# Element order of the squares in a group norm: from the token order to the order of the DRAM row

## The chip, the core and the metric

The kernel runs on one core of a Trainium2 chip. The metric is the device time of one execution in microseconds (us), from the first to the last instruction and what lies around it. The engines named below are TensorE (PE; its loads of the stationary operand are listed apart as PEld), VectorE (DVE), ScalarE (ACT), GpSimd (POOL) and SyncE (SP, which issues DMAs).

## The reference, cut to what matters

One decoder block: two token mixers (dilated attention, and a Mamba-2 state-space mixer), a gated merge, and an MLP, for 512 tokens of width 1024 in float32. The change touches the end of the state-space mixer, where the output of each of 8 groups (256 channels) is gated, and normalised by the mean of its squares over the 256 channels of the group:

```python
y = y.reshape(b, s, SSM_INNER) * jax.nn.silu(z.astype(jnp.float32))
yg = y.reshape(b, s, SSM_GROUPS, SSM_INNER // SSM_GROUPS)
yg = yg * lax.rsqrt(jnp.mean(yg * yg, axis=-1, keepdims=True) + RMS_EPS)
y = yg.reshape(b, s, SSM_INNER) * norm_w.astype(jnp.float32)
```

## The kernel before, in words

All projections run on TensorE, with both operands split into a rounded part ("h") and a rest ("l"), as three matmuls per 128x128 block of weights: 128 rows by 512 tokens each. TensorE executes its instructions in the order of the program: `mm` and `tr` (lines 227 and 230) pin every one.

The state-space mixer takes the 8 groups in turn. `ssm_group(g, sz)` is a generator of seven steps; the loop that drives it puts matmuls of the next projections (`fill`: x, B and C, z, and the output projection of the group before) between two steps, a fixed number of them. In the fourth step of a group, for each half j of its channels (128 channels on the partitions, 512 tokens in the free dimension), DVE makes the gated output y (lines 831 to 839) and ACT writes its squares, divided by 256, to a tile q (line 841). DVE adds the two tiles of squares into the first (line 844). Then come 10.5 us worth of other matmuls by the kernel's own count (`SSM_FILL`), and in the fifth step TensorE sums the squares over the partitions: four matmuls whose stationary operand is 128 of the 512 columns of squares and whose moving operand is one column of ones, so that the sums land in a PSUM tile `pn` with 128 tokens on the partitions and 4 columns. Each of these float32 matmuls is two instructions in the trace, and each has a load of its own: 64 loads and 64 matmuls in the 8 groups.

Column c of `pn` holds the tokens 4t + c, t being the partition: so the stationary operand of column c is every fourth element of the 512 (`by4`). The order is there for what follows: DVE adds epsilon to `pn` (line 212), POOL raises it to the power -1/2 (line 215), a DMA writes the [128, 4] tile to a row in DRAM, where t and c together are the token in order, and a second DMA reads that row back to all partitions, where DVE scales y by it (line 864).

ACT's squares are pinned to the order of the program, as are all of TensorE's instructions. Where the addition on DVE (line 844) and the evacuations around it stand on their engines is the scheduler's choice.

Of the kernel before, what the change touches and what calls it, by code (L numbers as in the profile page):

```python
# [13 lines left out]
AF = mybir.ActivationFunctionType  # L14
# [4 lines left out]
P = 128  # L19
T = 512  # L20
NT = 4
# [16 lines left out]
UC = 256  # L38
# [45 lines left out]
def hybrid_block(ctx: ExitStack, tc: tile.TileContext, a: dict):  # L84
    nc = tc.nc
    act, dve, pool, pe, sp = nc.scalar, nc.vector, nc.gpsimd, nc.tensor, nc.sync
# [8 lines left out]
    def split(src, hi, lo, eng=None, pinned=False, lo_pinned=False):  # L95
        ins = act.activation(hi, src, AF.Copy)  # L96
        if pinned:
            tc.keep_in_program_order(ins)
        ins = (eng or dve).tensor_tensor(lo, src, hi.bitcast(F32), op=ALU.subtract)  # L99
        if lo_pinned:  # L100
            tc.keep_in_program_order(ins)
# [107 lines left out]
    def rstd_of(dst, ms, ms2=None):  # L209

        if ms2 is None:
            dve.tensor_scalar(dst, ms, EPS, None, ALU.add)
        else:
            dve.tensor_scalar(dst, ms, ms2, EPS, ALU.add, ALU.add)
        pool.tensor_tensor(dst, dst, mhalf.broadcast_to(list(dst.shape)), op=ALU.pow)

    ones = const.tile([P, P], F32, name="ones")
# [5 lines left out]
    def pin(ins):  # L223
        return tc.keep_in_program_order(ins)

    def mm(*args, **kw):
        tc.keep_in_program_order(pe.matmul(*args, **kw))  # L227

    def tr(dst, src):
        tc.keep_in_program_order(pe.transpose(dst, src, ident))  # L230
# [4 lines left out]
    def three(ps, wh, wl, uh, ul, start, stop, w_moving=False):  # L235
        if w_moving:
            mm(ps, uh, wh, start=start, stop=False)
            mm(ps, uh, wl, start=False, stop=False)
            mm(ps, ul, wh, start=False, stop=stop)
        else:  # L240
            mm(ps, wh, uh, start=start, stop=False)
            mm(ps, wh, ul, start=False, stop=False)
            mm(ps, wl, uh, start=False, stop=stop)
# [14 lines left out]
    def abank(name):  # L258
        return psa.tile([P, T], F32, name=name, tag="a")
# [18 lines left out]
    with tc.tile_pool(name="start", bufs=1, reuse_waits="tile") as st:  # L278
# [163 lines left out]
        t = [vp.tile([P, GROUPS, NT, HG], F32, name=f"dt{j}") for j in range(4)]  # L442
# [185 lines left out]
    for key in ATT_UNITS:  # L628
        n, j = key[:-1], int(key[-1])
# [70 lines left out]
    def bc64(t, g, c0=0, c1=NT):  # L700
        v = t[:, g * 16 + c0 * HG : g * 16 + c1 * HG]
        return v.unsqueeze(2).broadcast_to([P, (c1 - c0) * HG, 64])

    def h64(ap_):
        return ap_.rearrange("p (q e) -> p q e", e=64)
# [62 lines left out]
    def ssm_group(g, sz):  # L768

        xs2 = [convs.pop((g, c)) for c in range(2)]  # L770
        w, e = ws_e.pop(g)

        xd = sg.tile([P, NT * UC], F32, name=f"xd{g}", tag="xd")
        for b in range(2):
            pt = abank(f"ptx{g}_{b}")
            for c2 in range(2):
                c = 2 * b + c2
                for j, xx in enumerate(xs2):
                    tr(pt[:, c2 * UC + j * P : c2 * UC + (j + 1) * P], xx[:, c * P : (c + 1) * P])
            dve.tensor_tensor(h64(xd[:, b * T : (b + 1) * T]), h64(pt), bc64(dtc, g, 2 * b, 2 * b + 2), op=ALU.mult)  # L780
        xs = sg.tile([P, 3 * UC], F32, name=f"xs{g}", tag="prev")
        dve.tensor_tensor(h64(xs), h64(xd[:, : 3 * UC]), bc64(ds_, g, 0, 3), op=ALU.mult)
        xsp = [sg.tile([P, 3 * UC], F32R, name=f"xs{n}{g}", tag=f"xs{n}") for n in "hl"]
        split(xs, *xsp)
        yield

        bt, ct = convs.pop((g, 2)), convs.pop((g, 3))
        pb = abank(f"pb{g}")
        for c in range(3):
            tr(pb[:, c * P : (c + 1) * P], bt[:, c * P : (c + 1) * P])  # L790
        bk = [sg.tile([P, TC], F32R, name=f"bk{n}{g}", tag=f"bk{n}") for n in "hl"]
        split(pb[:, :TC], *bk)
        pcb = abank(f"pcb{g}")
        for c in range(NT):
            cs = slice(c * P, (c + 1) * P)
            mm(pcb[:, cs], bt[:, cs], ct[:, cs], start=True, stop=True)
        cbm = sg.tile([P, NT, P], F32, name=f"cbm{g}", tag="cbm")
        dve.tensor_tensor(cbm, pcb.rearrange("p (c l) -> p c l", c=NT), tri.unsqueeze(1).broadcast_to([P, NT, P]),
                          op=ALU.mult)
        for c in range(NT):  # L800
            wv = w[:, c * HG : (c + 1) * HG, :]
            dve.tensor_tensor(wv, wv, cbm[:, c, :].unsqueeze(1).broadcast_to([P, HG, P]), op=ALU.mult)
        yield

        prev = sg.tile([P, 3, UC], F32, name=f"prev{g}", tag="prev")
        pst = [abank(f"pst{g}_{b}") for b in range(2)]
        for c in range(3):
            pv = pst[c // 2][:, (c % 2) * UC : (c % 2 + 1) * UC]
            bs, us = slice(c * P, (c + 1) * P), slice(c * UC, (c + 1) * UC)
            three(pv, bk[0][:, bs], bk[1][:, bs], xsp[0][:, us], xsp[1][:, us], True, True)  # L810
        with tc.high_priority(offset=200):
            act.activation(prev[:, 0, :], pst[0][:, 0:UC], AF.Copy)
            for c in (1, 2):
                pv = pst[c // 2][:, (c % 2) * UC : (c % 2 + 1) * UC]
                pin(dve.tensor_tensor(h64(prev[:, c, :]), h64(prev[:, c - 1, :]), bc64(cd, g, c, c + 1), op=ALU.mult))
                pin(dve.tensor_tensor(prev[:, c, :], prev[:, c, :], pv, op=ALU.add))
        while held:
            held.pop()()
        yield

        ys, sq = [], []
        pyds = [abank(f"pyd{g}_{j}") for j in range(2)]
        for j in range(2):
            for c in range(NT):
                for half in range(2):
                    h = 2 * j + half
                    mm(pyds[j][64 * half : 64 * half + 64, c * P : (c + 1) * P],
                       xd[:, c * UC + h * 64 : c * UC + (h + 1) * 64], w[:, c * HG + h, :], start=True, stop=True)
        for j in range(2):
            y = sg.tile([P, T], F32, name=f"y{g}_{j}", tag="y", bufs=2)  # L830
            dve.scalar_tensor_tensor(y, xs2[j], dskip[:, 2 * g + j : 2 * g + j + 1], pyds[j], op0=ALU.mult, op1=ALU.add)
            pyo = abank(f"pyo{g}_{j}")
            for c in range(1, NT):
                mm(pyo[:, (c - 1) * P : c * P], prev[:, c - 1, j * P : (j + 1) * P], ct[:, c * P : (c + 1) * P],
                   start=True, stop=True)
            t1 = sg.tile([P, TC], F32, name=f"t1{g}_{j}", tag="t1", bufs=2)
            dve.tensor_tensor(t1, pyo[:, :TC], e[:, j, :], op=ALU.mult)
            dve.tensor_tensor(y[:, P:], y[:, P:], t1, op=ALU.add)
            dve.scalar_tensor_tensor(y, y, 0.5, sz[j], op0=ALU.mult, op1=ALU.mult)
            q = sg.tile([P, T], F32, name=f"sq{g}_{j}", tag="sq", bufs=2)  # L840
            pin(act.activation(q, y, AF.Square, scale=1.0 / math.sqrt(UC)))
            ys.append(y)
            sq.append(q)
        dve.tensor_tensor(sq[0], sq[0], sq[1], op=ALU.add)
        yield

        pn = abank(f"pn{g}")
        by4 = sq[0].rearrange("p (t c) -> p c t", c=NT)
        for c in range(NT):
            mm(pn[:, c : c + 1], by4[:, c, :], ones[:, 0:1], start=True, stop=True)  # L850
        rt = sg.tile([P, NT], F32, name=f"rt{g}", tag="rt", bufs=2)
        rstd_of(rt, pn[:, :NT])

        row = dram.tile([P, NT], F32, name=f"rt_d{g}")
        pool.dma_start(row, rt)
        rstd = sg.tile([P, T], F32, name=f"rg{g}", tag="rg")
        pool.dma_start(rstd, row.rearrange("(o t) c -> o (t c)", o=1).broadcast_to([P, T]))
        if g + 1 < GROUPS:
            decays(g + 1)
        yield  # L860
        yield
        yt = yts[g] = [sg.tile([P, 2, T], F32R, name=f"yt{n}{g}", tag=f"yt{n}", bufs=1) for n in "hl"]
        for j in range(2):
            pin(dve.scalar_tensor_tensor(ys[j], ys[j], nw[:, 2 * g + j : 2 * g + j + 1], rstd,
                                         op0=ALU.mult, op1=ALU.mult))
            split(ys[j], yt[0][:, j, :], yt[1][:, j, :])
# [501 lines left out]
```

## Time and profile before

| | |
|---|---|
| median of 3 runs | 1097.21 us (1097.13 to 1097.43) |
| the profiled execution | 1096.37 us |
| its span, first to last instruction | 1094.5 us |
| TensorE matmuls, share of the span | 99% |
| TensorE loads, share of the span | 85% |
| DVE, ACT, POOL, share of the span | 67%, 48%, 7% |
| mean granted clock of TensorE | 0.998 |

[...] What a stretch costs is read from the starts of its instructions.

### The profile page before, as it was taken

How to read it: one execution, taken by the hardware profiler on the slowest of the kernel's cores; microseconds unless marked ns; L12 is line 12 of the kernel's file. 1: busy time of each engine (PE TensorE's matmuls, PEld its weight loads, DVE VectorE, ACT ScalarE, POOL GpSimd, SP SyncE). 2: the span in 40 equal slices, each digit the busy share in tenths (PEclk: the TensorE clock that was granted, in tenths of full speed). 3: DMA queues.
4: the chain of work that ended last, by engine and by line, in shares of the span. 5: the costliest groups of instructions: out<-in, count | busy, mean ns of one | idle time of the engine just before them, and what ended most of it. 6: DMA issues, size and time to landing. Idle time of an engine off the chain costs nothing.

```text
span 1094.5 us, 14714 instructions
## 1 busy us (share of the span) xinstructions
PE 1083.4 (99%) x5959; PEld 929.5 (85%) x5959; DVE 730.9 (67%) x1088; ACT 527.9 (48%) x921; POOL 72.0 (7%) x87
## 2 busy tenths in 40 slices
PE   9999999999999999999999999999999999999997
PEld 8988887778888888888888878889899998888886
DVE  6557666446776879696969695868677886243324
ACT  6256656435374645546373623443467666232322
POOL 3203122000000000000000000000000000000000
PEclk9999999999999999999999999999999999999999
DMA  8232112323333332323324222560233323333202
GB/s 278 81 116 78 55 63 68 106 68 106 116 87 119 84 125 78 125 82 121 112 92 150 86 82 88 191 192 1 78 116 116 102 93 135 116 118 113 80 37 78
DMA packets 87653, 113.06 MB, mean 103 GB/s; under 512 B 4624, under 2 KB 74768, under 8 KB 86560
## 3 DMA queue, kind: packets, MB, share of 16 engines
q1 hardware_dynamic: 85216, 101.01, 28.7%
q0 software_dynamic: 2224, 11.09, 3.0%
q8 instruction: 47, 0.77, 0.3%
q14 instruction: 22, 0.18, 0.1%
q10 hardware_dynamic: 144, 0.00, 0.0%
HBM read 109.92 MB, written 2.18 MB: 102 GB/s over the span
## 4 chain that ended last, share of the span: by engine, by line
PE 95%; DVE 2%; DMA 1%; issue 1%; ACT 1%; SPq 0%; POOLq 0%; POOL 0%; DVEq 0%; ACTq 0%
PE psd L227 15%; PE psx L227 8%; PE psz L227 8%; PE psbc L227 8%; PE pssp L227 7%; PE psuX L227 6%; PE psu L227 4%; PE psga L227 4%; PE psgs L227 4%; PE psk L227 3%; PE psq L227 3%; PE psuZ L227 3%; PE psv L227 3%; PE psap L227 3%; PE psp L227 2%; PE pso L227 2%
## 5 line engine op out<-in xcount | busy, mean ns | idle before, releaser
L227 PE MATMUL psd<-wl_dn,hh 128*128 128x512 f32 x240 | 93.5, 390 | 0.0
L227 PE MATMUL psd<-wh_dn,hh 128*128 128x512 f32 x240 | 93.5, 390 | 0.0
L227 PE MATMUL psd<-wh_dn,hl 128*128 128x512 f32 x240 | 93.5, 389 | 0.0
L99 DVE TENSOR_TENSOR hl<-hidden,hh 128x512 fp32r<-128x512 f32 x31 | 21.1, 692 | 71.3 <-ACT hh L96 71.3
L96 ACT ACTIVATE hh<-hidden 128x512 fp32r<-128x512 f32 x31 | 19.1, 628 | 91.8 <-PE psd L227 91.8
L227 PEld LDWEIGHTS psd<-wh_dn,hh 128*128 128x128 f32 x240 | 45.1, 188 | 9.4
L227 PEld LDWEIGHTS psd<-wl_dn,hh 128*128 128x128 f32 x240 | 45.1, 188 | 9.3
L227 PEld LDWEIGHTS psd<-wh_dn,hl 128*128 128x128 f32 x240 | 45.1, 188 | 9.3
L693 DVE SCALAR_TENSOR_TENSOR ch<-psx,cw,ch 128x511 f32<-128x511 f32 (+2 forms) x48 | 35.9, 747 | 23.0 <-ACT ch L691 22.3
L227 PE MATMUL psz<-uh,wh_z 128*128 128x512 f32 x128 | 51.1, 399 | 0.0
L227 PE MATMUL pssp<-yth,wh_sp 128*128 128x512 f32 x128 | 50.9, 398 | 0.0
L227 PE MATMUL psx<-uh,wl_x 128*128 128x512 f32 x128 | 50.1, 392 | 0.7 <-DVE wl_x L99 0.7
L227 PE MATMUL psx<-uh,wh_x 128*128 128x512 f32 x128 | 50.6, 395 | 0.0
L227 PE MATMUL pssp<-yth,wl_sp 128*128 128x512 f32 x128 | 50.2, 392 | 0.0
L227 PE MATMUL psz<-uh,wl_z 128*128 128x512 f32 x128 | 50.1, 391 | 0.0
L227 PE MATMUL pssp<-ytl,wh_sp 128*128 128x512 f32 x128 | 50.0, 391 | 0.0
L227 PE MATMUL psbc<-uh,wh_bc 128*128 128x512 f32 x128 | 50.0, 390 | 0.0
L227 PE MATMUL psz<-ul,wh_z 128*128 128x512 f32 x128 | 50.0, 390 | 0.0
L227 PE MATMUL psbc<-uh,wl_bc 128*128 128x512 f32 x128 | 49.9, 390 | 0.0
L227 PE MATMUL psbc<-ul,wh_bc 128*128 128x512 f32 x128 | 49.8, 389 | 0.0
L227 PE MATMUL psx<-ul,wh_x 128*128 128x512 f32 x128 | 49.8, 389 | 0.0
L696 ACT ACTIVATE ct<-ch 128x512 f32<-128x512 f32 x32 | 20.0, 626 | 52.1 <-DVE ch L693 52.1
(360 smaller groups left out, 3267.4 us busy)
## 6 DMA issues: line engine op xcount, KB each, us to landing
ws_up<-in_w_up_dram SPq DMA_DIRECT2D x16, 1024.0 KB, 5.5
ws_dn<-in_w_down_dram SPq DMA_DIRECT2D x15, 1024.0 KB, 5.0
ws_z<-in_w_in_dram SPq DMA_DIRECT2D x8, 1024.0 KB, 7.1
ws_x<-in_w_in_dram SPq DMA_DIRECT2D x8, 1024.0 KB, 5.2
w<-acs_d POOLq DMA_DIRECT2D x8, 1024.0 KB, 5.6
ws_bc<-in_w_in_dram SPq DMA_DIRECT2D x16, 512.0 KB, 4.7
ws_sp<-in_w_ssm_proj_dram SPq DMA_DIRECT2D x8, 1024.0 KB, 4.9
ws_ga<-in_w_in_dram SPq DMA_DIRECT2D x4, 1024.0 KB, 5.8
```

The lines of the kernel that those rows point to most:

```text
L96: ins = act.activation(hi, src, AF.Copy)
L99: ins = (eng or dve).tensor_tensor(lo, src, hi.bitcast(F32), op=ALU.subtract)
L227: tc.keep_in_program_order(pe.matmul(*args, **kw))
L693: dve.scalar_tensor_tensor(h[:, d:], ps[:, : T - d], cw[:, ct, 3 - d : 4 - d], h[:, d:], op0=ALU.mult, op1=ALU.add)
L696: act.activation(t, h, AF.Tanh)
```

## The change

ACT now reads y in steps of four elements and writes the squares side by side, so that the tile of squares holds first the tokens 4t, then 4t + 1, and so on; the four stationary operands are then four runs of 128 adjacent elements. DVE's addition and everything from `pn` on work on the same values in the same places as before.

```diff
-            pin(act.activation(q, y, AF.Square, scale=1.0 / math.sqrt(UC)))
+
+            pin(act.activation(q.rearrange("n (c p) -> n c p", c=NT), y.rearrange("n (p c) -> n c p", c=NT), AF.Square,
+                               scale=1.0 / math.sqrt(UC)))
...
         pn = abank(f"pn{g}")
-        by4 = sq[0].rearrange("p (t c) -> p c t", c=NT)
         for c in range(NT):
-            mm(pn[:, c : c + 1], by4[:, c, :], ones[:, 0:1], start=True, stop=True)
+            mm(pn[:, c : c + 1], sq[0][:, c * P : (c + 1) * P], ones[:, 0:1], start=True, stop=True)
```

## Rows read from the trace of the kernel before

Groups of the state-space mixer are counted from 0 to 7; the times of a group are those of its own stretch of the trace, in us from the start of the span.

**Rows 1.** The page: the span, the busy time of the engines, TensorE's granted clock in 40 slices, and the chain of work that ended last, by engine.

```profile
span 1094.5 us, 14714 instructions
PE 1083.4 (99%) x5959; PEld 929.5 (85%) x5959; DVE 730.9 (67%) x1088; ACT 527.9 (48%) x921; POOL 72.0 (7%) x87
PEclk9999999999999999999999999999999999999999
PE 95%; DVE 2%; DMA 1%; issue 1%; ACT 1%; SPq 0%; POOLq 0%; POOL 0%; DVEq 0%; ACTq 0%
```

**Rows 2.** The stretch of the eight groups, 242 to 665 us: all that TensorE waited for (total, times, longest), and the piece of the chain that the sums of group 3 are (start, us, what).

```profile
PE pyd L227 <- DVE w L802: 0.8, 2, 0.6
PE psx L227 <- DVE wl_x L99: 0.7, 1, 0.7
...
451.53 1.63 PE pn L227 x8
```

**Rows 3.** Busy time by engine in one group's stretch (start:end, us, then busy us and instructions of each engine, granted clock, DMA share, GB/s).

```profile
404.00:456.00 52.00, 52.00 (x273) 43.87 (x272) 42.44 (x63) 26.12 (x47) 2.73 (x4) 1.00 0.34 107
```

**Rows 4.** Groups of TensorE's loads by shape (count | busy us, mean ns of one | idle before): those of the sums, and those of `pcb`, another float32 matmul of the same loop whose stationary operand is 128 adjacent elements.

```profile
L227 PEld LDWEIGHTS pn<-ones,sq 128*128 128x128 f32 x64 | 15.5, 324 | 0.3
L227 PEld LDWEIGHTS pcb<-ct,ct 128*128 128x128 f32 x64 | 7.8, 192 | 0.0
```

**Rows 5.** Timeline around the sums of group 0, first loads, then matmuls (start us, us, what, count). A row of x8 spans eight instructions.

```profile
300.27 1.94 PEld L227 LDWEIGHTS pn<-ones,sq 128*128 128x128 f32 x8
302.12 0.21 PEld L227 LDWEIGHTS psbc<-uh,wh_bc 128*128 128x128 f32 x1
302.25 0.19 PEld L227 LDWEIGHTS psbc<-ul,wh_bc 128*128 128x128 f32 x1
...
300.04 0.39 PE L227 MATMUL psbc<-ul,wh_bc 128*128 128x512 f32 x1
300.27 0.40 PE L227 MATMUL psbc<-uh,wl_bc 128*128 128x512 f32 x1
300.50 1.80 PE L227 MATMUL pn<-ones,sq 128*128 128x1 f32 x8
302.16 0.48 PE L227 MATMUL psbc<-uh,wh_bc 128*128 128x512 f32 x1
302.48 0.39 PE L227 MATMUL psbc<-ul,wh_bc 128*128 128x512 f32 x1
```

**Rows 6.** Timeline of the loads of `pcb` in group 0 and of the two loads after them.

```profile
275.53 0.97 PEld L227 LDWEIGHTS pcb<-ct,ct 128*128 128x128 f32 x8
276.42 0.19 PEld L227 LDWEIGHTS psap<-ah,wh_ap 128*128 128x128 f32 x1
276.53 0.19 PEld L227 LDWEIGHTS psap<-al,wh_ap 128*128 128x128 f32 x1
```

**Rows 7.** Groups of ACT's instructions by shape: the squares (512 elements), and two others of 1024 and 2048, all on adjacent elements.

```profile
L841 ACT ACTIVATE sq<-y 128x512 f32<-128x512 f32 x16 | 10.1, 632 | 70.5 <-DVE y L839 70.3
L96 ACT ACTIVATE wh_z<-ws_z 128x1024 fp32r<-128x1024 f32 x16 | 16.8, 1049 | 2.0 <-PE psga L227 1.1 <-PE psx L227 0.9
L765 ACT ACTIVATE w<-w 128x2048 f32<-128x2048 f32 x8 | 15.3, 1909 | 0.1
```

**Rows 8.** Timeline from the last gated output of group 3 to its sums: DVE, ACT, TensorE's loads, TensorE (the bracket: idle time of the engine before, and who ended it).

```profile
448.56 0.69 DVE L839 SCALAR_TENSOR_TENSOR y<-y,sz 128x512 f32<-128x512 f32 x1
449.95 0.69 DVE L844 TENSOR_TENSOR sq<-sq,sq 128x512 f32<-128x512 f32 x1 [0.70 <-ACT sq L841]
453.25 0.16 DVE L212 TENSOR_SCALAR rt<-pn 128x4 f32<-128x4 f32 x1 [1.50 <-PE pn L227]
...
449.29 0.63 ACT L841 ACTIVATE sq<-y 128x512 f32<-128x512 f32 x1 [2.75 <-DVE y L839]
450.20 0.78 ACT L691 ACTIVATE ch<-psx,cb,cw 128x512 f32<-128x512 f32 x1 [0.28 <-PE psx L227]
...
451.13 1.94 PEld L227 LDWEIGHTS pn<-ones,sq 128*128 128x128 f32 x8
...
451.36 1.80 PE L227 MATMUL pn<-ones,sq 128*128 128x1 f32 x8
```

**Rows 9.** The addition on DVE in group 0 (its sums are in rows 5), and the addition and the first load of the sums in groups 2 and 6, the first and the last of five groups with the same distance between the two.

```profile
295.38 0.68 DVE L844 TENSOR_TENSOR sq<-sq,sq 128x512 f32<-128x512 f32 x1
...
397.85 0.69 DVE L844 TENSOR_TENSOR sq<-sq,sq 128x512 f32<-128x512 f32 x1 [0.70 <-ACT sq L841]
399.03 0.31 PEld L227 LDWEIGHTS pn<-ones,sq 128*128 128x128 f32 x1
...
606.25 0.69 DVE L844 TENSOR_TENSOR sq<-sq,sq 128x512 f32<-128x512 f32 x1 [0.70 <-ACT sq L841]
607.43 0.31 PEld L227 LDWEIGHTS pn<-ones,sq 128*128 128x128 f32 x1
```

**Rows 10.** The same in the last group, 7, where ACT takes both squares back to back.

```profile
658.56 1.24 ACT L841 ACTIVATE sq<-y 128x512 f32<-128x512 f32 x2 [2.08 <-DVE y L839]
...
660.37 0.68 DVE L844 TENSOR_TENSOR sq<-sq,sq 128x512 f32<-128x512 f32 x1
...
662.44 1.94 PEld L227 LDWEIGHTS pn<-ones,sq 128*128 128x128 f32 x8
```

**Rows 11.** A place where TensorE did wait for DVE: two instructions of line 802 (one of them alone takes 0.68 us, first row) and the matmul that waited for the first of the two.

```profile
646.87 0.68 DVE L802 TENSOR_TENSOR w<-w,cbm 128x512 f32<-128x512 f32 x1
648.39 1.28 DVE L802 TENSOR_TENSOR w<-w,cbm 128x512 f32<-128x512 f32 x2
...
649.13 0.44 PE L227 MATMUL pyd<-w,xd 128*64 128x128 f32 x4 [0.61 <-DVE w L802]
```

## The prediction

> **What bounds the kernel now.** [...] A group takes some 52 us, in which TensorE is busy without a gap while DVE has work for 42 us and ACT for 26 [rows 3]; in all eight groups together TensorE waits 1.5 us for others [rows 2]. So what shortens TensorE's own work here shortens the kernel, as long as no other engine becomes late. [...]
>
> [...] One load is recorded with 324 ns, while a load of the same 128 columns for `pcb` has 192 ns [rows 4]. The starts say what that costs, since loads and matmuls overlap. The eight loads of the sums begin at 300.27, the load after them at 302.12, and the one after that at 302.25 [rows 5]. The first of the eight hides behind a matmul of 512 columns: the matmul of 300.27 is followed by the first of the sums at 300.50, at the usual distance of 0.23 us (300.04 to 300.27) [rows 5]. From 300.50 on nothing covers the loads: seven intervals up to 302.12 are 1.62 us, 0.23 us each. The eight loads of `pcb` go from 275.53 to 276.42, that is 0.11 us each [rows 6]. The stationary operand of the sums is every fourth element, that of `pcb` is adjacent elements; the rest of the form is alike.
>
> **The change part by part: the loads.** What is an adjacent load worth right behind a matmul of one column? The trace has one such place: the load at 302.12 is of adjacent elements, stands behind the last of the sums, and the next follows 0.13 us later [rows 5]. After `pcb`, whose matmuls move 128 columns, the same distance is 0.11 (276.42 to 276.53) [rows 6]. I take 0.11 for the first of the seven intervals, which stands behind the first matmul of the sums with its load already hidden, and 0.13 for the other six: 0.89 us in place of 1.62, so 0.73 us less in a group, and 8 x 0.73 = 5.8 us in all. With 0.11 throughout it would be 8 x (1.62 - 0.77) = 6.8 us; with 0.15, a little above the dearest adjacent load seen, 8 x (1.62 - 1.05) = 4.6 us.
>
> Does it reach the end? Behind the sums stand matmuls of the projection in progress, ready to run: the next begins right at 302.16 [rows 5]. DVE's instruction for `pn` has waited 1.50 us for the sums in group 3, with other DVE work queued behind it [rows 8]; it comes earlier too. What the other engines do after the sums is released by TensorE's own progress and moves with it. The sums' result goes through POOL and two DMAs, which start earlier by the same amount. No DMA is added or moved, and none passes another in a queue. I count the 0.73 us as kept whole.
>
> **The squares on ACT.** They now read in steps of 16 bytes and write adjacent elements. The trace shows no ACT instruction that reads single elements in steps, so its price X above the present 0.63 us needs bounds. From below it is zero, not less: the same 512 elements pass, and adjacent reading is already the best that any row shows. ACT spends (1909 - 1049)/1024 = 0.84 ns on an element [rows 7], 0.43 us on 512. The nearest row of a stepped read of the same memory is the loads' own: 0.23 against 0.11 us, twice the time. Twice on ACT is X = 0.43 us, and this I take. Four times (X = 1.29 us) I keep as the upper bound, since ACT may have less to hide such a read behind than TensorE has.
>
> [...]
>
> Sixteen squares at 0.43 us are 6.9 us more ACT work, beside 26 of 52 us busy in a group. What matters is who waits for it: DVE's addition, and behind it the first load of the sums. In group 3 the second square starts when y is done (448.56 + 0.69 = 449.25, ACT at 449.29), the addition follows at 449.95 and ends at 450.64; the first load of the sums starts at 451.13 and its matmul at 451.36 [rows 8]. So the addition ends only 0.49 us ahead of the load, in groups 2 to 6 alike [rows 9]. From the end of a DVE instruction to the matmul that waits for it is 0.06 us (648.39 + 0.68 = 649.07, then 649.13) [rows 11], and an adjacent load needs 0.13 before its matmul. The addition may thus end at 451.36 - 0.13 - 0.06 = 451.17, 0.53 us later than now. X = 0.43 fits under it with 0.10 to spare, and costs nothing; that is the cover, and without it each of the five groups would lose X. Group 0 has 4.2 us between the addition's end and the load [rows 5, 9]. In group 7 ACT takes both squares in a row, done at 659.80, and the addition starts only at 660.37 for another reason; it may end 1.43 us later than 661.05, so up to 2X = 1.96 is free there [rows 10]. Behind the square on ACT an evacuation of `psx` starts 0.28 us after it could [rows 8]; it slips by 0.15 us, and DVE's work behind it stands ahead of a wait for the sums anyway. DVE's addition costs the same, adjacent in and out.
>
> **The sum.** 5.8 us less and nothing back: the profiled execution of 1096.37 us, whose span is 1094.5, would come to 1090.6. The median of the runs is 0.84 above that execution, so the median to expect is 1097.21 - 5.8 = 1091.4 us, 0.53% less. Anything within 0.2%, 2.2 us, counts as the same, about what a measurement of this kernel can tell from no change.
>
> **The rivals.** First, ACT's stepped read is dearer than the cover, and TensorE waits where it never waited. The loss is 5 x (X - 0.53) us, and from X = 0.98 on also 2X - 1.96 for group 7. At four times the element price, X = 1.29, it is 3.8 + 0.6 = 4.4 us, and the time 1095.8. The gain is gone at X = 1.50, and from X = 1.81, which is 4.4 ns for an element, the kernel is slower by 0.2% or more: 1099.4 and up. For it speaks that 0.10 us to spare is little and that the price is not in the trace; against it, that five times the present price of an element would be needed, where the loads show twice. A weaker form of the same is that the scheduler, which places DVE's addition, now puts another DVE instruction such as one of 0.69 us ahead of it: 0.43 + 0.69 - 0.53 = 0.59 in five groups, 3.0 us, so 1094.4.
>
> Second, the loads do not get shorter, because it is the matmul of one column that holds them up and not the step. The time stays at 1097.2. For it: no row shows eight adjacent loads behind matmuls of one column. Against it: the 0.13 us of the adjacent load at 302.12, and the recorded length, 324 against 192 ns, of the load itself [rows 4, 5]. [...]
>
> **How the numbers follow.** The forecast, X under the cover or just over it, has a chance of 0.72: 1090.4 to 1092.6 by the bounds of an adjacent load (6.8 and 4.6 us). The first rival in its mild form (X up to 1.1, or another instruction ahead of the addition), 1092.6 to 1095.0, has 0.09. Harder, up to no gain or a small loss, 0.04; slower by over 0.2%, 0.06, with other mishaps on ACT's path. Loads that stay long, 1097.2, 0.09. So faster 0.81, same 0.13, slower 0.06. The range reaches from the lower bound, 1090.2, over the mild rival to 1095.2.
>
> **What would show it.** In the profile after: loads of `pn` at some 190 ns; from the second load of the sums to the first load after them 0.9 us in place of 1.62; squares of about 1.06 us; the addition ending some 0.07 us before the first load; no wait of TensorE for line 844; the distance of two groups' sums some 0.7 us shorter. The prediction is wrong if the loads stay at 0.23 us, if TensorE waits for the squares, or if the groups' gain is there and a later stage gives it back.

## The result, and the profile after

| | before | after |
|---|---|---|
| median | 1097.22 us (1097.13 to 1097.43, 4 runs) | 1090.42 us (1089.61 to 1090.63, 4 runs) |
| the profiled execution | 1096.37 us | 1089.61 us |
| its span | 1094.5 us | 1087.8 us |

The ratio is 0.9936 (95% interval 0.9919 to 0.9954): 6.8 us or 0.62% by the medians, where 5.8 us had been forecast. The direction, the place and the mechanism are those of the prediction. The gain had been put too low by 1.0 us, and the time lies at the lower edge of the range: 0.2 us above it by the median, and 0.01 below it if the ratio is applied to 1097.21.

The page after: the span, the engines' busy time, and the squares, which now rank among the costliest groups.

```profile
span 1087.8 us, 14714 instructions
PE 1076.3 (99%) x5959; PEld 921.3 (85%) x5959; DVE 731.0 (67%) x1088; ACT 534.7 (49%) x921; POOL 72.0 (7%) x87
...
L842 ACT ACTIVATE sq<-y 128x512 f32<-128x512 f32 x16 | 17.8, 1120 | 70.5 <-DVE y L839 70.4
```

The loads of the sums by shape (count | busy us, mean ns | idle before), and all that TensorE's matmuls waited for between 242 and 665 us:

```profile
L227 PEld LDWEIGHTS pn<-ones,sq 128*128 128x128 f32 x64 | 8.4, 191 | 0.6
```

```profile
PE pyd L227 <- DVE w L802: 0.8, 2, 0.6
PE psx L227 <- DVE wl_x L99: 0.7, 1, 0.7
```

The recorded load has gone from 324 to 191 ns, the length of other adjacent loads [rows 4], and the waits are those of before [rows 2]. ACT's square has gone from 632 to 1120 ns [rows 7]: X, left open in the prediction, is 0.49 us.

The timeline around the sums of group 0, loads and then matmuls, answers to [rows 5]:

```profile
300.31 1.08 PEld L227 LDWEIGHTS pn<-ones,sq 128*128 128x128 f32 x8
301.31 0.19 PEld L227 LDWEIGHTS psbc<-uh,wh_bc 128*128 128x128 f32 x1
301.42 0.19 PEld L227 LDWEIGHTS psbc<-ul,wh_bc 128*128 128x128 f32 x1
...
300.30 0.39 PE L227 MATMUL psbc<-uh,wl_bc 128*128 128x512 f32 x1
300.53 0.95 PE L227 MATMUL pn<-ones,sq 128*128 128x1 f32 x8
301.34 0.48 PE L227 MATMUL psbc<-uh,wh_bc 128*128 128x512 f32 x1
301.66 0.39 PE L227 MATMUL psbc<-ul,wh_bc 128*128 128x512 f32 x1
```

The first matmul of the sums starts 0.23 us after the one before it, as in the kernel before: its load is hidden. The seven intervals behind it go from 300.53 to 301.31, 0.78 us or 0.11 each, where they were 1.62. And the load after the sums is followed by the next after 0.11 us, where it was 0.13. From the last matmul ahead of the sums to the second one behind them is now 1.36 us (300.30 to 301.66), before 2.21 (300.27 to 302.48 in [rows 5]): 0.85 us a group, 6.8 us in eight.

Group 3 answers to [rows 8]: ACT, DVE, loads, matmuls.

```profile
446.72 1.11 ACT L842 ACTIVATE sq<-y 128x512 f32<-128x512 f32 x1 [2.75 <-DVE y L839]
...
447.86 0.69 DVE L846 TENSOR_TENSOR sq<-sq,sq 128x512 f32<-128x512 f32 x1 [1.17 <-ACT sq L842]
449.84 0.16 DVE L212 TENSOR_SCALAR rt<-pn 128x4 f32<-128x4 f32 x1 [0.56 <-PE pn L227]
...
448.61 1.05 PEld L227 LDWEIGHTS pn<-ones,sq 128*128 128x128 f32 x8
...
448.56 0.40 PE L227 MATMUL psx<-uh,wl_x 128*128 128x512 f32 x1
448.80 0.95 PE L227 MATMUL pn<-ones,sq 128*128 128x1 f32 x8
...
449.92 0.39 PE L227 MATMUL psx<-ul,wh_x 128*128 128x512 f32 x1
```

Here the other side of the change is seen. The addition ends at 447.86 + 0.69 = 448.55, and the first load follows 0.05 us later (unrounded); before, it had 0.49 us to spare. The load now waits for the addition: it starts 0.04 us after the matmul that hides it (448.61 against 448.56, unrounded 0.042), where it used to start with it. The matmul behind it starts 0.24 us after its neighbour in place of 0.23. So the cover was used almost whole, and it held. DVE's own wait for the sums has shrunk from 1.50 to 0.56 us.

### The profile page after: what moved, and what is told of

The parts are those of the page before. It is cut to its first block, busy times and chain, and to the rows that moved or that the text cites. A ratio compares the mean times of both kernels' runs of the same rounds, so it can differ in the third digit from the quotient of the medians.

```text
span 1087.8 us, 14714 instructions
## 1 busy us (share of the span) xinstructions
PE 1076.3 (99%) x5959; PEld 921.3 (85%) x5959; DVE 731.0 (67%) x1088; ACT 534.7 (49%) x921; POOL 72.0 (7%) x87
## 4 chain that ended last, share of the span: by engine, by line
PE 92%; DVE 4%; DMA 2%; ACT 1%; issue 1%; POOL 0%; SPq 0%; POOLq 0%; DVEq 0%; ACTq 0%
PE psd L227 16%; PE psx L227 8%; PE psz L227 8%; PE psbc L227 8%; PE pssp L227 7%; PE psuX L227 6%; PE psu L227 4%; PE psga L227 4%; PE psgs L227 4%; PE psk L227 3%; PE psq L227 3%; PE psuZ L227 3%; PE psv L227 3%; PE psap L227 3%; PE psuY L227 1%; PE pq L227 1%
## 5 line engine op out<-in xcount | busy, mean ns | idle before, releaser
L842 ACT ACTIVATE sq<-y 128x512 f32<-128x512 f32 x16 | 17.8, 1120 | 70.5 <-DVE y L839 70.4
```

The costliest lines, as they stand in the source:

```text
L842: pin(act.activation(q.rearrange("n (c p) -> n c p", c=NT), y.rearrange("n (p c) -> n c p", c=NT), AF.Square, scale=1.0 / math.sqrt(UC)))
```

## The experiments

The edits are shown against the changed kernel (that of one pass, token order, against one pass); what each leaves wrong in the sums is said in its expectation. Times on several chips are compared by their ratio to the kernel before, run beside them (median 1096.70 us for the runs of the first table, 1096.86 for the second). The start of the kernel scatters between executions, by up to 0.8 us at the first sums, so the mechanism is read in each group from its own starts.

| run | median, us | ratio to the kernel before (95%) |
|---|---|---|
| loads only | 1089.42 | 0.9932 (0.9917 to 0.9946) |
| read only | 1097.05 | 1.0002 (0.9992 to 1.0011) |
| late square | 1091.04 | 0.9946 (0.9931 to 0.9960) |
| one pass | 1086.66 | 0.9906 (0.9891 to 0.9921) |

| run | median, us | ratio to the kernel before (95%) |
|---|---|---|
| step on the write | 1089.83 | 0.9936 (0.9921 to 0.9951) |
| DVE permutes | 1089.71 | 0.9934 (0.9918 to 0.9951) |
| one pass, token order | 1089.33 | 0.9931 (0.9917 to 0.9946) |
| steps (a probe, one run) | 1093.29 | |

**Loads only.** The half of the change that was to bring the gain, without its price.

```diff
-            pin(act.activation(q.rearrange("n (c p) -> n c p", c=NT), y.rearrange("n (p c) -> n c p", c=NT), AF.Square,
-                               scale=1.0 / math.sqrt(UC)))
+            pin(act.activation(q, y, AF.Square, scale=1.0 / math.sqrt(UC)))
```

> ACT writes the squares in the token order again, TensorE still takes four runs of 128 adjacent elements (so the sums belong to other tokens than the row in DRAM says). Theory: the whole gain is the loads' own, 0.112 us for each of seven intervals in place of 0.23, and 0.02 at the load behind them; then this kernel is as fast as the changed one, 6.8 us below the kernel before (1090.4), the addition ends 0.5 us ahead of the first load, and the first of the sums starts 0.23 us after the matmul before it in every group. Rival, ACT's stepped read costs a part of it already: then this kernel is faster than the changed one by that part, 0.5 us or more. Rival, the order on ACT made the gain: then this kernel stays at 1097.2.

The theory holds: 0.9932 beside 0.9936. DVE's addition, the loads in group 3, and the matmuls just ahead of the sums of groups 3 and 4:

```profile
447.52 0.69 DVE L845 TENSOR_TENSOR sq<-sq,sq 128x512 f32<-128x512 f32 x1 [0.70 <-ACT sq L842]
...
448.70 1.08 PEld L227 LDWEIGHTS pn<-ones,sq 128*128 128x128 f32 x8
449.70 0.19 PEld L227 LDWEIGHTS psx<-uh,wh_x 128*128 128x128 f32 x1
...
448.70 0.39 PE L227 MATMUL psx<-uh,wl_x 128*128 128x512 f32 x1
...
499.90 0.39 PE L227 MATMUL psx<-uh,wl_x 128*128 128x512 f32 x1
```

The addition ends at 448.21, again 0.49 us ahead of the load, and the eight loads take the 1.00 us that they take in the changed kernel where nothing delays the first (300.31 to 301.31). The two ratios differ by some 0.4 us, which the intervals can't tell from nothing; the trace can tell a part of it. From the matmul ahead of the sums of group 3 to that of group 4 are 51.21 us here (448.70 to 499.90, unrounded) and 51.25 in the changed kernel (448.56 to 499.82); before there were 52.10. The same 0.05 us lies between the two kernels from group 2 to group 6, and the kernel in which DVE permutes has 51.21 too. So ACT's stepped read did cost the changed kernel something, some 0.05 us in each of five groups or 0.2 us in all; less than 0.01 us of it lies in the sums, the rest in the first dozen matmuls behind them, and why it lies there no run here shows.

**Read only.** The other half alone.

```diff
-            mm(pn[:, c : c + 1], sq[0][:, c * P : (c + 1) * P], ones[:, 0:1], start=True, stop=True)
+            mm(pn[:, c : c + 1], sq[0].rearrange("p (t c) -> p c t", c=NT)[:, c, :], ones[:, 0:1], start=True, stop=True)
```

> ACT reads in steps as in the changed kernel, TensorE's stationary operand is every fourth element again (so the sums belong to other tokens). Theory: the seven intervals are 0.23 us again, and the squares of 1.12 us end the addition 0.49 us later, at the start of the first load; a stepped load is recorded with 0.31 us, so the first of the sums starts some 0.14 us late in groups 2 to 6, 0.7 us in all: 1097.9. By the working on record, where only the time that a load occupies counts (0.21 us), 0.04 us a group and 1097.4. Rival, the gain comes with ACT: 1090.4.

1.0002: nothing gained, as both readings had it, so the gain lies in the loads alone. Group 3, loads and matmuls:

```profile
452.04 1.94 PEld L227 LDWEIGHTS pn<-ones,sq 128*128 128x128 f32 x8
453.88 0.21 PEld L227 LDWEIGHTS psx<-uh,wh_x 128*128 128x128 f32 x1
454.01 0.19 PEld L227 LDWEIGHTS psx<-ul,wh_x 128*128 128x128 f32 x1
...
452.00 0.40 PE L227 MATMUL psx<-uh,wl_x 128*128 128x512 f32 x1
452.23 1.84 PE L227 MATMUL pn<-ones,sq 128*128 128x1 f32 x8
...
454.24 0.39 PE L227 MATMUL psx<-ul,wh_x 128*128 128x512 f32 x1
```

From 452.00 to 454.24 are 2.24 us, 0.04 us more than the 2.21 of before; in groups 2, 4, 5 and 6 it is 0.04 to 0.05 us more, in groups 0, 1 and 7 nothing. Of the two prices that stood in the expectation, 0.14 us by the recorded length of a load and 0.04 by the time that it occupies, the second is right: my theory there was the worse of the two. And the distance of 0.13 us behind the last stepped load is back (453.88 to 454.01), though the load measured is adjacent. It goes with the stepped load ahead of it. That is the row from which the prediction took its price.

**Late square.** One more ACT instruction ahead of the second square, to see what lies behind the cover.

```diff
+            if j == 1:
+                pin(act.activation(q[:, :P], y[:, :P], AF.Square, scale=1.0 / math.sqrt(UC)))
             pin(act.activation(q.rearrange("n (c p) -> n c p", c=NT), y.rearrange("n (p c) -> n c p", c=NT), AF.Square,
                                scale=1.0 / math.sqrt(UC)))
```

> The changed kernel with one more ACT instruction ahead of the second square of each group: a square of 128 elements, whose result is written over. It takes ACT some 0.3 us (rows of 128 elements are recorded with 0.39, and neighbours overlap). Theory: in groups 2 to 6 the addition ends 0.05 us before the first load in the changed kernel, nothing is left, so each of these five groups loses the full 0.3 us: 1.5 us, 1091.9, with TensorE's loads waiting for the addition in those five groups and not in groups 0, 1 and 7. Rival, there is cover left (the recorded load hides the wait): no change from 1090.4. Rival, ACT's other work behind it is delayed too and costs more: 1093 or above.

Group 3 (ACT, matmuls), and the wait of TensorE's loads for the addition in the whole stretch (total, times, longest):

```profile
447.57 0.31 ACT L843 ACTIVATE sq<-y 128x128 f32<-128x128 f32 x1 [2.75 <-DVE y L839]
447.91 1.11 ACT L844 ACTIVATE sq<-y 128x512 f32<-128x512 f32 x1
...
449.42 0.39 PE L227 MATMUL psx<-uh,wl_x 128*128 128x512 f32 x1
449.80 1.05 PE L227 MATMUL pn<-ones,sq 128*128 128x1 f32 x8
...
451.04 0.40 PE L227 MATMUL psx<-ul,wh_x 128*128 128x512 f32 x1
```

```profile
PEld pn L227 <- DVE sq L848: 2.1, 5, 0.4
```

The group's second square starts at 447.91; without the added one it would have started at 447.57, 0.34 us earlier. The stretch from 449.42 to 451.04 is 1.62 us, 0.26 more than the 1.36 of the changed kernel; five groups make 1.3 us, and TensorE's loads wait for the addition in just those five. The theory of a used-up cover holds but for a remainder of 0.08 us a group. Together with the 0.49 us that the changed kernel takes, the cover is some 0.57 us, against 0.53 worked out on record. By the ratios the run is 1.1 us slower than the changed kernel, in intervals that overlap; the trace carries the verdict.

**One pass.** Fewer loads of the same price (`ones_r` is a copy of the ones in the rounded format).

```diff
-        dve.tensor_tensor(sq[0], sq[0], sq[1], op=ALU.add)
+        total = sg.tile([P, T], F32R, name=f"sqs{g}", tag="sqs", bufs=1)
+        dve.tensor_tensor(total, sq[0], sq[1], op=ALU.add)
...
-            mm(pn[:, c : c + 1], sq[0][:, c * P : (c + 1) * P], ones[:, 0:1], start=True, stop=True)
+            mm(pn[:, 2 * c : 2 * c + 2], total[:, c * P : (c + 1) * P], ones_r[:, 0:2], start=True, stop=True)
```

The copy `ones_r` is made once, ahead of the loop (left out here); `rstd_of` then reads every second column of `pn`.

> The changed kernel with the added squares rounded to the format in which the projections' operands stand, so that each of the four sums is one matmul (of two equal columns) and one load in place of two. The squares lose low bits by that. Theory: TensorE's time for the sums is the number of loads by 0.112 us; four fewer in a group are 0.45 us, 3.6 us in eight groups: 1086.8. Rival, a load of this format is dearer behind so short a matmul, up to 0.19 us as recorded: 4 x 0.19 in place of 8 x 0.112 saves 0.14 us a group, 1.1 us: 1089.3. Rival, another engine is the bound by now and the gain is not kept: 1090.4.

**One pass, token order.** The same in the order of before, with ACT adjacent.

```diff
-            pin(act.activation(q.rearrange("n (c p) -> n c p", c=NT), y.rearrange("n (p c) -> n c p", c=NT), AF.Square,
-                               scale=1.0 / math.sqrt(UC)))
+            pin(act.activation(q, y, AF.Square, scale=1.0 / math.sqrt(UC)))
...
+        by4 = total.rearrange("p (t c) -> p c t", c=NT)
...
-            mm(pn[:, 2 * c : 2 * c + 2], total[:, c * P : (c + 1) * P], ones_r[:, 0:2], start=True, stop=True)
+            mm(pn[:, 2 * c : 2 * c + 2], by4[:, c, :], ones_r[:, 0:2], start=True, stop=True)
```

> The kernel before with one matmul and one load for each of the four sums, the added squares rounded as in the run before with four loads, but in the token order, with stepped loads and ACT reading adjacent elements. Theory: the sums cost TensorE the number of its loads by their price; with four stepped loads in place of eight, 4 x 0.233 = 0.93 us less in a group, 7.5 us in all, 1089.3 to 1089.7, a ratio of 0.9932; the step costs 4 x 0.12 x 8 = 3.9 us against the run with four adjacent loads (0.9906). Rival: a stepped load of the rounded format has another price (twice that of the adjacent one is what the theory says); at the adjacent price it would be 0.9906 here as well.

Both came out as the theory has it, 0.9906 and 0.9931. The loads of group 0, first the adjacent four, then the stepped four:

```profile
300.45 0.64 PEld L229 LDWEIGHTS pn<-ones_r,sqs 128*128 128x128 f32 x4
301.00 0.19 PEld L229 LDWEIGHTS psbc<-uh,wh_bc 128*128 128x128 f32 x1
301.12 0.19 PEld L229 LDWEIGHTS psbc<-ul,wh_bc 128*128 128x128 f32 x1
```

```profile
300.55 1.01 PEld L229 LDWEIGHTS pn<-ones_r,sqs 128*128 128x128 f32 x4
301.46 0.21 PEld L229 LDWEIGHTS psbc<-uh,wh_bc 128*128 128x128 f32 x1
301.59 0.19 PEld L229 LDWEIGHTS psbc<-ul,wh_bc 128*128 128x128 f32 x1
```

With the first interval hidden (0.23), three are left: 0.55 - 0.23 = 0.32 us, 0.11 each, and 0.91 - 0.23 = 0.68, 0.23 each. The sums cost the number of their loads by 0.11 or 0.23 us, in the rounded format as in the full one (0.78 us for the seven intervals of the changed kernel, 1.62 before). Halving the loads and making them adjacent are two gains of nearly the same size, and in the time of the sums, loads times price, they multiply: the first of these two runs is the fastest kernel here, at a ratio 0.0030 below the changed one's, with the added squares rounded.

**Step on the write, and DVE permutes.** The same permutation at two other places.

```diff
-            pin(act.activation(q.rearrange("n (c p) -> n c p", c=NT), y.rearrange("n (p c) -> n c p", c=NT), AF.Square,
+            pin(act.activation(q.rearrange("n (c p) -> n p c", c=NT), y.rearrange("n (p c) -> n p c", c=NT), AF.Square,
```

> The changed kernel, but ACT reads y in the token order and writes in steps of 128 elements; the same values in the same places. Theory: a stepped write has no reason to be dearer for ACT than a stepped read, 1.12 us or less, and anything up to 1.12 us is covered: as fast as the changed kernel, a ratio of 0.9936 to the kernel before. If the write is free (0.63 us), the addition ends 0.5 us ahead of the load again and the ratio is that of the loads alone, 0.9932. Rival: a write in steps is dearer than a read; every 0.1 us over 1.12 costs 0.08 us in each of five groups, so 1.6 us for a square would cost 2 us.

```diff
-            pin(act.activation(q.rearrange("n (c p) -> n c p", c=NT), y.rearrange("n (p c) -> n c p", c=NT), AF.Square,
-                               scale=1.0 / math.sqrt(UC)))
+            pin(act.activation(q, y, AF.Square, scale=1.0 / math.sqrt(UC)))
...
-        dve.tensor_tensor(sq[0], sq[0], sq[1], op=ALU.add)
+        total = sg.tile([P, T], F32, name=f"sqs{g}", tag="sqs", bufs=1)
+        dve.tensor_tensor(total.rearrange("n (c p) -> n c p", c=NT), sq[0].rearrange("n (p c) -> n c p", c=NT),
+                          sq[1].rearrange("n (p c) -> n c p", c=NT), op=ALU.add)
...
-            mm(pn[:, c : c + 1], sq[0][:, c * P : (c + 1) * P], ones[:, 0:1], start=True, stop=True)
+            mm(pn[:, c : c + 1], total[:, c * P : (c + 1) * P], ones[:, 0:1], start=True, stop=True)
```

> ACT's squares are adjacent in and out as in the kernel before; DVE's addition reads both tiles in steps of four elements and writes a tile of its own in the order of the DRAM row; the loads are adjacent. Theory: DVE pays for the step as ACT does, about 1 ns an element more, 0.69 us become 1.2; the addition then ends where it does in the changed kernel, and the ratio is 0.9936. If two stepped sources cost DVE twice that, 1.7 us, five groups lose 0.4 us each, and DVE has 8 x 1 us more work: 0.9955. Rival: the step costs DVE nothing, 0.9932.

The squares with a stepped write, and DVE's addition with two stepped sources, by shape:

```profile
L842 ACT ACTIVATE sq<-y 128x512 f32<-128x512 f32 x16 | 18.2, 1149 | 70.5 <-DVE y L839 70.3
```

```profile
L846 DVE TENSOR_TENSOR sqs<-sq,sq 128x512 f32<-128x512 f32 x8 | 8.6, 1074 | 4.7 <-ACT sq L842 4.7
```

A step on ACT's write costs 1149 ns, about what one on its read does; DVE's addition goes from 0.69 us to 1.07, 0.38 more. All three places fit under the cover, and the times of the three kernels can't be told apart (0.9936 for the changed one, 0.9936, 0.9934). The rival of a write dearer than the read is out.

**Steps.** A probe of the price by step (`load_view`, `read_view` and `write_view`, left out here, pick the elements that the expectation lists).

```diff
-            mm(pn[:, c : c + 1], sq[0][:, c * P : (c + 1) * P], ones[:, 0:1], start=True, stop=True)
+            mm(pn[:, c : c + 1], load_view(sq[0], c), ones[:, 0:1], start=True, stop=True)
...
+            pin(act.activation(write_view(q), read_view(y), AF.Square, scale=1.0 / math.sqrt(UC)))
```

> A probe in the place of the squares: the eight groups take different steps (the sums are then of other elements and mean nothing). Loads: group 0 adjacent, 1 every second, 2 every third, 3 every fourth element, 4 adjacent from an odd element, 6 every second from an odd one, and 5 and 7 every sixth and fifth element of the tile of decays. ACT reads: adjacent in group 0, then steps of 2, 8 and 4 elements in groups 1, 2, 3, runs of two in 4 and in 8 elements in groups 4 and 5, runs of four in 16 in group 6, steps of 16 in group 7; writes adjacent. [...] Rival, every step other than adjacent costs the same: 0.23 and 1.12 at step 2 too. Rival, the price grows with the step: over 0.23 at 5 and 6, over 1.12 at 8 and 16.

The eight loads of a group and the load after them, in groups 1 (step 2), 2 (step 3), 3 (step 4) and 7 (step 5):

```profile
347.34 1.13 PEld L227 LDWEIGHTS pn<-ones,sq 128*128 128x128 f32 x8
348.39 0.19 PEld L227 LDWEIGHTS psx<-uh,wh_x 128*128 128x128 f32 x1
...
398.01 1.47 PEld L227 LDWEIGHTS pn<-ones,sq 128*128 128x128 f32 x8
399.39 0.20 PEld L227 LDWEIGHTS psx<-uh,wh_x 128*128 128x128 f32 x1
...
449.68 1.95 PEld L227 LDWEIGHTS pn<-ones,sq 128*128 128x128 f32 x8
451.54 0.21 PEld L227 LDWEIGHTS psx<-uh,wh_x 128*128 128x128 f32 x1
...
659.18 1.85 PEld L227 LDWEIGHTS pn<-ones,e 128*128 128x128 f32 x8
660.93 0.21 PEld L227 LDWEIGHTS psgs<-uh,wh_gs 128*128 128x128 f32 x1
```

A load at step 2 takes (348.39 - 347.34 - 0.23)/7 = 0.12 us. In groups 2 and 3 the squares come so late that the first load is not hidden whole, so the division is by eight: 1.38/8 = 0.17 at step 3, 1.86/8 = 0.23 at step 4. Step 5 is (1.75 - 0.23)/7 = 0.22, no dearer than 4. The interval behind the eight loads, which was 0.13 us behind stepped ones, goes with the step as well: 0.11 at step 2, 0.12 at step 3, 0.13 at steps 4 to 6. ACT's reads, the second square of groups 1 (step 2), 2 (step 8), 3 (step 4), 4 (runs of two in four) and 5 (runs of two in eight):

```profile
339.41 0.65 ACT L859 ACTIVATE sq<-y 128x512 f32<-128x512 f32 x1
...
396.06 1.17 ACT L859 ACTIVATE sq<-y 128x512 f32<-128x512 f32 x1 [2.75 <-DVE y L856]
...
447.80 1.11 ACT L859 ACTIVATE sq<-y 128x512 f32<-128x512 f32 x1 [2.75 <-DVE y L856]
...
499.94 0.67 ACT L859 ACTIVATE sq<-y 128x512 f32<-128x512 f32 x1 [2.74 <-DVE y L856]
...
551.19 0.69 ACT L859 ACTIVATE sq<-y 128x512 f32<-128x512 f32 x1 [2.75 <-DVE y L856]
```

Single elements at 4 or 8 cost ACT 1.11 to 1.17 us (at 16 the two squares of group 7 take 1.10 and 1.13); step 2 costs nearly the adjacent price (0.65 beside 0.63), and so do runs of two (0.67 and 0.69). Both rivals fall: step 2 is nearly free for the loads (0.12 us beside 0.11) and for ACT, and steps beyond 4 are no dearer for the loads (0.22 at 5, and at 6 by the eight of group 5, from 553.04 to 554.80) and hardly for ACT (1.17 at 8 beside 1.11 at 4). What sets these prices no run here shows.

## Why the prediction came out as it did, step by step

- **TensorE bounds the stretch, and what it saves in the sums reaches the end:** right. What TensorE's matmuls waited for is unchanged (0.8 and 0.7 us), and the gain is there with the loads alone (0.9932) and absent without them (1.0002).
- **The price of an adjacent load behind a matmul of one column: the step that failed.** I took 0.13 us for six of the seven intervals, from the one adjacent load that stood behind the stepped ones. It measured 0.11 in all seven, the price of the loads of `pcb`, which I had kept as the upper bound of the gain. Read only shows why the row misled: the 0.13 returns with the stepped loads, though the load measured is adjacent, and in the probe it goes with the step of the load ahead (0.11 to 0.13). So that interval was no price of the new kind alone, and it too fell to 0.11. The seven intervals went from 1.61 to 0.78 us by the loads' own starts, so 0.83 + 0.02 = 0.85 us a group in place of 0.73, and 6.8 us in place of 5.8. Where those 0.02 us come from no run here shows.
- **The upper bound of the gain** was 6.8 us for the seven intervals; the end of the range stood 0.2 us below the time that it gives, and executions of the changed kernel alone differ by 1.0 us. The range was too tight on that side.
- **ACT's price X:** 0.49 us measured, 0.43 taken from the loads' ratio, which was near. The ratio itself held: an element went to 2.1 times its price on ACT ((0.43 + 0.49)/0.43), as on the loads. That it would carry from one engine to another was not known, and DVE shows that it need not: 0.69 us became 1.07 there.
- **The cover of 0.53 us:** right, some 0.57 by the late square. The change lived on it: X left less than 0.1 us a group. That X costs nothing under it was not quite so: some 0.05 us in each of the five groups (loads only), 0.2 us of 6.8.
- **The first rival,** a dear read that makes TensorE wait: its mechanism is real (late square: 0.26 us in each of the five groups named, none in the others), its condition was not met. Its weaker form did not arise: DVE's addition stands where it stood.
- **The second rival,** loads that stay long because of the one-column matmul: out. Behind the same matmuls of one column a load of 128 columns took 0.11, 0.12, 0.17 and 0.23 us at steps 1 to 4.

## What to carry to other kernels

A stationary operand of every fourth, fifth or sixth float32 element loaded at half the rate here (0.22 to 0.23 us for 128 columns against 0.11), and behind these sums' matmuls, of one or two columns, nothing hid that: count such loads, and move the step to an engine with time to spare. What that engine then pays has to fit between its end and the moment TensorE asks, and that distance, read from the starts of both, decided more here than the engine's busy share: ACT was busy for half of a group's time, yet had some 0.57 us to give. For a price, prefer a row whose neighbours are also of the new kind; an interval next to an operation of the old kind may differ from one among the new (0.13 us here against 0.11).

## What the runs showed of the hardware that was not expected

Three engines paid for the same permutation, each its own price: TensorE's load 0.12 us more for 128 columns (0.23 against 0.11), ACT 0.49 us more for 512 elements (1120 ns on the read and 1149 on the write against 632, about 1 ns an element), DVE 0.38 us more for 512 with both sources stepped (1074 ns against 693). On ACT neither the step alone nor adjacent neighbours alone told the price: 512 elements in steps of two, and in adjacent pairs at four or eight, took 0.65 to 0.70 us beside 0.63, and single elements at steps of 4, 8 and 16 took 1.10 to 1.20. And a load of the rounded format took the same 0.11 us as each of the two loads of a full float32 matmul; what made the full format dearer in these sums was the number of its loads, eight a group against four.
